# One-hot matrices of token tile 0 moved to ScalarE, and a product and two casts of the routing moved to GpSimd, in an encoder block on one Trainium2 core

## The chip, the core and the metric

The kernel runs on one core of a Trainium2 chip. The metric is the device time of one execution in microseconds (us), the median of the runs shown. The core's engines are TensorE (PE, with its weight loads as PEld), VectorE (DVE), ScalarE (ACT), GpSimd (POOL) and SyncE (SP); each runs its own instructions in the order in which the program lists them and waits for the others by semaphores. A gather of table rows is an indirect DMA that GpSimd issues.

## The reference

One layer: a normalised input goes through two mixers (gated linear attention and differential softmax attention), whose outputs are merged and added. Then comes the part that the change touches, a retrieval layer over 128 x 128 experts, each a row of two tables:

```python
s = einsum('thpc,hpnc->thpn', qb, sub_keys)        # 2 scores per head over 128 keys
sv, si = top_k(s, 16)                              # for each of the two halves
cand = sv[:, :, 0, :, None] + sv[:, :, 1, None, :] # 16 x 16 sums
cidx = si[:, :, 0, :, None] * 128 + si[:, :, 1, None, :]
cv, ci = top_k(cand, 16)
eidx = take_along_axis(cidx, ci)                   # 16 experts of 16384 for a token and head
g = softmax(cv)
a = gelu(einsum('thkd,td->thk', u_tab[eidx], x))   # dot of the token with 16 rows of u
out = einsum('thk,thkd->td', g * a, v_tab[eidx])   # weighted sum of 16 rows of v
```

There are 256 tokens, 8 heads and rows of 2048 numbers, all in 32 bits. Each token so needs 128 rows of each table.

## The kernel before

The 256 tokens are two tiles (`tt` 0 and 1) of 128, one token to a partition. After the mixers come eight `queries(h)`: a projection, scores, and `route(0, h, ...)`, which finds the 16 experts of each token of tile 0 for head h. `route` is a chain of small VectorE instructions: `top16` twice over 128 scores and once over the 256 sums, a cast of the indices (`sif`), shifts and a mask (`hl`), a cast (`hlf`), a comparison that makes one-hot rows (`ohx`, 128x512), a product of these with `sif`, a sum (`ijt`), and the expert's number (`ent`). `route(1, h, ...)` for tile 1 follows in a second loop.

`gather_dots(tt, h, ei)` makes 16 pairs: an indirect DMA on GpSimd that brings one row of the u table to each partition (1 MB), and a VectorE instruction (line 754, "a dot" below) that multiplies it with the tokens and sums. The rows land in buffers of two rings of three, tiles `g` (pool `ring`) and `gr` (tag `raw` of pool `wp`), by turns; a gather waits until the dot that read its buffer last is done. There are 128 gathers and dots for a tile, 256 in all.

`weights_of(tt)` waits for all 128 dots of its tile, applies Gelu on ScalarE, and transposes the expert's numbers and weights to `slotT` (a column for each token). Then 32 calls of `build_w` make W0, a 128x128 matrix for each of the 128 tokens of tile 0, four tokens a call. For a token one engine makes the one-hot row of the first index times the weight (`oi`, VectorE, line 815), another that of the second index (`oj`, GpSimd, line 816), TensorE multiplies the two (line 817), and ScalarE copies four products from PSUM to W0 (line 818). These calls are written after the gathers and dots of tile 1, four calls to a head, and share VectorE's and GpSimd's queues with them. `build_w1` makes W1 for tile 1 later by like means, in part on ScalarE (lines 828 and 829); then W0 and W1 are multiplied with the whole v table (`dense_v`), while 576 of the 2048 columns come by gathers.

The program doesn't set the order of instructions by hand: a scheduler with costs of its own orders each engine's queue when the kernel is built, so that a change of one instruction's engine moves others.

Of the kernel before, what the change touches and what calls it, by code (L numbers as in the profile page):

```python
# [10 lines left out]
F32 = mybir.dt.float32  # L11
# [4 lines left out]
AF = mybir.ActivationFunctionType  # L16
ALU = mybir.AluOpType
# [3 lines left out]
P = 128  # L21
# [19 lines left out]
def block_kernel(ctx: ExitStack, tc: tile.TileContext, A: dict, out: bass.AP):  # L41
    nc = tc.nc

    def pool(name, bufs=1, space=None, side=None, c=ctx):
        kw = {}
        if space is not None:
            kw["space"] = space
        if side is not None:
            kw["side"] = side
        return c.enter_context(tc.tile_pool(name=name, bufs=bufs, **kw))  # L50
# [5 lines left out]
    wp = pool("wp", side="right", c=wpc)  # L56
# [4 lines left out]
    bt = pool("bt")  # L61
# [9 lines left out]
    def pa(shape):  # L71
        return paux.tile(list(shape), F32, tag="pa", name="pa")
# [15 lines left out]
    iota = cc[:, 128:256]  # L88
    onec = cc[:, 256:257]
# [59 lines left out]
    for k in range(KT):  # L149
        ps = pa([P, N])  # L150
# [78 lines left out]
    for kh in range(2):  # L229
        raw = bt.tile([P, 8, 32], F32, tag="ow", name="lraw", bufs=4)  # L230
        nc.sync.dma_start(raw, w_lr[kh])
        hi = wp.tile([P, 8, P], F32R, tag="hi", name="lhi", bufs=3)
# [416 lines left out]
    for j in range(8):  # L649
# [10 lines left out]
        for b in range(2):  # L660
# [3 lines left out]
            for tt in range(2):  # L664
# [4 lines left out]
                                           op1=ALU.subtract)  # L669
# [36 lines left out]
    def top16(vo, io, src, n):  # L706
        tmp = rp.tile([P, n], F32, tag=f"tk{n}", name="tk", bufs=1)
        nc.vector.max(vo[:, 0:8], src)
        nc.vector.max_index(io[:, 0:8], vo[:, 0:8], src)
        nc.vector.match_replace(tmp, vo[:, 0:8], src, NEG)  # L710
        nc.vector.max(vo[:, 8:16], tmp)
        nc.vector.max_index(io[:, 8:16], vo[:, 8:16], tmp)

    def route(tt, h, s_):

        sv = rp.tile([P, 2, 16], F32, tag="sv", name="sv", bufs=2)
        si = rp.tile([P, 2, 16], U32, tag="si", name="si", bufs=2)
        for p in range(2):
            top16(sv[:, p, :], si[:, p, :], s_[:, p, :], P)
        sif = rp.tile([P, 2, 16], F32, tag="sif", name="sif", bufs=2)  # L720
        nc.vector.tensor_copy(sif, si)
        cand = rp.tile([P, 16, 16], F32, tag="cand", name="cand", bufs=1)
        nc.vector.tensor_tensor(cand, sv[:, 0, :].unsqueeze(2).to_broadcast([P, 16, 16]),
                                sv[:, 1:2, :].to_broadcast([P, 16, 16]), op=ALU.add)
        cv = rp.tile([P, 16], F32, tag="cv", name="cv", bufs=2)
        ci = rp.tile([P, 16], U32, tag="ci", name="ci", bufs=2)
        top16(cv, ci, cand.rearrange("p a b -> p (a b)"), 256)
        hl = rp.tile([P, 2, 16], U32, tag="hl", name="hl", bufs=2)
        nc.vector.tensor_scalar(hl[:, 0, :], ci, 4, None, op0=ALU.logical_shift_right)
        nc.vector.tensor_scalar(hl[:, 1, :], ci, 15, None, op0=ALU.bitwise_and)  # L730
        hlf = rp.tile([P, 2, 16], F32, tag="hlf", name="hlf", bufs=2)
        nc.vector.tensor_copy(hlf, hl)
        ohx = rp.tile([P, 2, 16, 16], F32, tag="ohx", name="ohx", bufs=1)
        nc.vector.tensor_tensor(ohx, hlf.unsqueeze(3).to_broadcast([P, 2, 16, 16]),  # L734
                                iota16.unsqueeze(1).unsqueeze(1).to_broadcast([P, 2, 16, 16]), op=ALU.is_equal)
        nc.vector.tensor_tensor(ohx, ohx, sif.unsqueeze(2).to_broadcast([P, 2, 16, 16]), op=ALU.mult)
        nc.vector.tensor_reduce(ij[tt][:, :, h * 16:(h + 1) * 16], ohx, axis=AX.X, op=ALU.add)
        ei = eit[:, tt, h]
        nc.vector.scalar_tensor_tensor(ei, ij[tt][:, 0, h * 16:(h + 1) * 16], 128.0,
                                       ij[tt][:, 1, h * 16:(h + 1) * 16], op0=ALU.mult, op1=ALU.add)  # L740
        nm = rp.tile([P, 1], F32, tag="nm", name="nm", bufs=2)
        nc.vector.tensor_scalar(nm, cv[:, 0:1], -1.0, None, op0=ALU.mult)
        nc.scalar.activation(gw[tt][:, h * 16:(h + 1) * 16], cv, AF.Exp, bias=nm, accum_out=gsum[tt][:, h:h + 1])
        return ei

    def gather_dots(tt, h, ei):
        for k in range(16):
            i = ngather[0]
            ngather[0] += 1
            g = ring.tile([P, D], F32, tag="g", name="g") if i % 2 else wp.tile([P, D], F32, tag="raw", name="gr", bufs=3)  # L750
            nc.gpsimd.indirect_dma_start(out=g, out_offset=None, in_=u_tab,  # L751
                                         in_offset=bass.IndirectOffsetOnAxis(ap=ei[:, k:k + 1], axis=0))
            s = h * 16 + k
            nc.vector.scalar_tensor_tensor(g, g, 1.0, xb[:, tt, :], op0=ALU.mult, op1=ALU.mult,  # L754
                                           accum_out=dots[tt][:, s:s + 1])

    def weights_of(tt):

        rc = rp.tile([P, 8], F32, tag="rcs", name="rcs", bufs=2)
        nc.vector.reciprocal(rc, gsum[tt])  # L760
        g3 = gw[tt].rearrange("p (h k) -> p h k", k=16)
        nc.vector.tensor_mul(g3, g3, rc.unsqueeze(2).to_broadcast([P, 8, 16]))
        nc.scalar.activation(dots[tt], dots[tt], AF.Gelu)
        nc.vector.tensor_mul(gw[tt], gw[tt], dots[tt])  # L764
        ps = pa([P, 3, P])
        nc.tensor.transpose(ps[:, 0, :], ij[tt][:, 0, :], ident)
        nc.tensor.transpose(ps[:, 1, :], ij[tt][:, 1, :], ident)
        nc.tensor.transpose(ps[:, 2, :], gw[tt], ident)  # L768
        r = bt.tile([P, 3, P], F32, tag=f"b{2 + tt}", name=f"slotT{tt}")
        nc.scalar.activation(r, ps, AF.Copy)  # L770
        return r
# [6 lines left out]
    def queries(h):  # L778
        qt = bt.tile([P, 2, T], F32, tag=f"b{2 + h % 2}", name="pqt")

        def ev_pq(b, ps):
            with tc.high_priority():
                nc.scalar.activation(qt[:, b, :], ps, AF.Copy)
        proj(w_q, h * 256, hg, T, ev_pq, lo_eng=nc.vector if h == 0 else nc.gpsimd, ring=wait[h])
        s0 = rp.tile([P, 2, P], F32, tag="sS0", name="sS0", bufs=2)
        with tc.high_priority():
            for tt in range(2):
                ps = pa([P, 2, P])
                for p in range(2):
                    nc.tensor.matmul(ps[:, p, :], lhsT=qt[:, p, tt * P:(tt + 1) * P], rhs=skT[h // 2][:, 2 * (h % 2) + p, :],  # L790
                                     start=True, stop=True)
                nc.scalar.activation(s0 if tt == 0 else sS1[:, h], ps, AF.Copy, scale=rst[tt])
            eis[0, h] = route(0, h, s0)
# [12 lines left out]
    W1E = "pav"  # L806


    def build_w(wt, sT, t4, oj_eng):
        ps = pa([P, 4, P])  # L810
        for q in range(4):
            t = t4 * 4 + q
            oij = bt.tile([P, 2, P], F32, tag="ow", name="oij", bufs=4)
            oi, oj = oij[:, 0, :], oij[:, 1, :]
            nc.vector.tensor_scalar(oi, iota, sT[:, 0, t:t + 1], sT[:, 2, t:t + 1], op0=ALU.is_equal, op1=ALU.mult)
            oj_eng(q).tensor_scalar(oj, iota, sT[:, 1, t:t + 1], None, op0=ALU.is_equal)  # L816
            nc.tensor.matmul(ps[:, q, :], lhsT=oj, rhs=oi, start=True, stop=True)  # L817
        nc.scalar.activation(wt[:, t4 * 4:t4 * 4 + 4, :], ps, AF.Copy)

    def build_w1(vp, wt, sT, nj, t4):  # L820
# [23 lines left out]
    for h in range(8):  # L844
        gather_dots(0, h, eis[0, h])
        eis[1, h] = route(1, h, sS1[:, h])
    w0p = pool("w0p")
    W0 = w0p.tile([P, P, P], F32, name="W0")
    sT0 = weights_of(0)
    for h in range(8):  # L850
        gather_dots(1, h, eis[1, h])
        for t4 in range(4 * h, 4 * h + 4):
            build_w(W0, sT0, t4, lambda q: nc.gpsimd)
    sT1 = weights_of(1)
    ringc.close()
    rgt.close()
# [183 lines left out]
```

## Time and profile before

| | |
|---|---|
| median of 3 runs | 2719.2 us (2715.19 to 2728.39) |
| the profiled execution's own time | 2721.86 us |
| its span in the profile | 2720.1 us |
| busy share of the span | PE 71%, DVE 82%, ACT 37%, POOL 48% |
| mean granted TensorE clock | 0.849 |
| moved by DMA | 659.14 MB, mean 242 GB/s |

Shares are means over the whole span. The routing and the gathers of the u table lie between about 1170 and 2057 us; what an instruction costs there is read from stretches of that time. One dot shows as two instructions in a count, the product (2.29 us) and a short read of the accumulator.

### The profile page before, as it was taken

To read this page: it belongs to the slowest core of one execution; us is meant where nothing else is said; L and a number is where in the kernel's file an instruction comes from. 1 tells how busy PE (TensorE), PEld (TensorE's weight loads), DVE (VectorE), ACT (ScalarE), POOL (GpSimd) and SP (SyncE) were. 2 spreads that over 40 slices of the span, in tenths; PEclk is the share of its full clock that TensorE was granted. 3 is DMA by queue.
4 is the path that set the end of the run, shared out by engine and by line. 5 is a ranking of instruction groups with operands and counts; after the bars stand their busy time and mean duration, and the time that the engine had idled before them with its cause. 6 is when DMAs were issued, how large, how long until landed. Compare 5 with 4: busy or idle time off the path is not lost.

```text
span 2720.1 us, 37043 instructions
## 1 busy us (share of the span) xinstructions
PE 1930.7 (71%) x13809; PEld 1847.4 (68%) x13809; DVE 2236.7 (82%) x3227; ACT 1009.3 (37%) x1790; POOL 1297.3 (48%) x1070
## 2 busy tenths in 40 slices
PE   8999999999999999987000002332006899999997
PEld 7999999999999999977000002221006888888886
DVE  4878887557777765589999997667988999999998
ACT  4555544345555444532000000000006445555444
POOL 1333310001100000076546889999865766667775
PEclk9999999999999999998555555555558899999999
DMA  4444445544444656645999997667993788888886
GB/s 168 142 156 156 167 160 186 186 174 160 163 164 170 218 186 224 225 178 201 344 353 349 363 412 299 212 216 290 421 371 136 256 288 296 298 288 299 289 294 232
DMA packets 111056, 659.14 MB, mean 242 GB/s; under 512 B 14530, under 2 KB 17148, under 8 KB 53260
## 3 DMA queue, kind: packets, MB, share of 16 engines
q0 software_dynamic: 59216, 348.40, 34.7%
q1 hardware_dynamic: 51456, 308.21, 32.6%
q8 instruction: 109, 1.79, 0.3%
q14 instruction: 71, 0.58, 0.1%
q10 hardware_dynamic: 204, 0.17, 0.0%
HBM read 653.53 MB, written 2.10 MB: 241 GB/s over the span
## 4 chain that ended last, share of the span: by engine, by line
DVE 21%; POOL 15%; issue 14%; DMA 3%; PE 3%; ACT 0%; POOLq 0%; DVEq 0%; ACTq 0%
DVE g L754 5%; DVE hs L884 4%; POOL gr L751 3%; POOL oij L816 3%; DVE gr L754 3%; POOL gv L881 3%; POOL g L751 3%; DMA gv<-in_peer_v_dram,ent 2%; POOL vlo L905 2%; PE pa L817 1%; DVE vlo L907 1%; DVE wv L896 1%; DVE oi L839 1%; DVE ohx L734 1%; PE acc L913 1%
## 5 line engine op out<-in xcount | busy, mean ns | idle before, releaser
L186 DVE TENSOR_TENSOR lo<-raw,hi 128x1024 fp32r<-128x1024 f32 x354 | 453.0, 1281 | 243.4 <-ACT hi L185 241.7
L202 PE MATMUL pm<-hT,lo 128*128 128x256 f32 (+1 forms) x2048 | 577.1, 285 | 7.9 <-DVE lo L186 7.9
L200 PE MATMUL pm<-hT,hi 128*128 128x256 f32 (+1 forms) x2048 | 581.2, 285 | 0.0
L201 PE MATMUL pm<-hT,hi 128*128 128x256 f32 (+1 forms) x2048 | 581.0, 284 | 0.0
L185 ACT ACTIVATE hi<-raw 128x1024 fp32r<-128x1024 f32 x374 | 395.6, 1059 | 354.5 <-PE pm L201 285.8
L202 PEld LDWEIGHTS pm<-hT,lo 128*128 128x128 f32 x2048 | 384.2, 189 | 10.7 <-DVE lo L186 9.0
L200 PEld LDWEIGHTS pm<-hT,hi 128*128 128x128 f32 x2048 | 385.4, 188 | 0.3
L201 PEld LDWEIGHTS pm<-hT,hi 128*128 128x128 f32 x2048 | 385.4, 188 | 0.2
L913 PE MATMUL acc<-vlo,wv 128*128 128x368 f32 x1024 | 348.9, 349 | 41.3 <-DVE vlo L905 19.2
L881 POOL DMA_INDIRECT gv<-in_peer_v_dram,ent x256 | 298.1, 1165 | 166.5 <-DVE hs L884 120.1
L768 PE MATMUL pa<-cc,gwt 128*128 128x128 f32 x2 | 1.0, 476 | 466.4 <-DVE gwt L764 466.4
L914 PE MATMUL acc<-vhi,wv 128*128 128x368 f32 x1024 | 331.8, 333 | 0.0
L768 PEld LDWEIGHTS pa<-cc,gwt 128*128 128x128 f32 x2 | 0.4, 183 | 467.1 <-DVE gwt L764 467.1
L754 DVE SCALAR_TENSOR_TENSOR g<-g,xb 128x2048 f32<-128x2048 f32 x128 | 308.0, 2409 | 10.0 <-DMA g<-in_peer_u_dram,ent 9.9
L754 DVE SCALAR_TENSOR_TENSOR gr<-gr,xb 128x2048 f32<-128x2048 f32 x128 | 292.4, 2286 | 21.3 <-DMA gr<-in_peer_u_dram,ent 21.1
L884 DVE SCALAR_TENSOR_TENSOR hs<-gv,gwt,hs 128x576 f32<-128x576 f32 x256 | 289.9, 1133 | 11.7 <-DMA gv<-in_peer_v_dram,ent 11.5
L751 POOL DMA_INDIRECT gr<-in_peer_u_dram,ent x128 | 240.6, 1879 | 97.7 <-DVE gr L754 44.4
L751 POOL DMA_INDIRECT g<-in_peer_u_dram,ent x128 | 236.2, 1845 | 103.3 <-DVE g L754 46.1
L913 PEld LDWEIGHTS acc<-vlo,wv 128*128 128x128 f32 x1024 | 193.3, 190 | 82.9 <-DVE vlo L905 42.4
L895 ACT ACTIVATE wv<-W 128x128 fp32r<-128x128 f32 x256 | 109.7, 430 | 311.6 <-DVE g L754 131.8
L912 PE MATMUL acc<-vhi,wv 128*128 128x368 f32 x1024 | 217.2, 334 | 1.2 <-ACT wv L895 1.1
L914 PEld LDWEIGHTS acc<-vhi,wv 128*128 128x128 f32 x1024 | 193.6, 190 | 0.0
(872 smaller groups left out, 4332.7 us busy)
## 6 DMA issues: line engine op xcount, KB each, us to landing
raw<-in_c_w_in_dram SPq DMA_DIRECT2D x128, 1024.0 KB
raw<-in_c_w_branch_gla_dram SPq DMA_DIRECT2D x16, 1024.0 KB
raw<-in_c_w_branch_diff_dram SPq DMA_DIRECT2D x16, 1024.0 KB
raw<-in_c_w_out_dram SPq DMA_DIRECT2D x16, 1024.0 KB
raw<-in_c_peer_w_q_dram SPq DMA_DIRECT2D x11, 1024.0 KB
gv<-in_peer_v_dram,ent POOLq DMA_INDIRECT x256
raws<-in_c_peer_w_q_dram SPq DMA_DIRECT2D x12, 256.0 KB
xt<-in_x_dram SPq DMA_DIRECT2D x2, 1024.0 KB
```

The lines of the kernel that those rows point to most:

```text
L185: nc.scalar.activation(hi[:, ks], raw, AF.Copy)
L186: (lo_eng or nc.vector).tensor_sub(lo[:, ks], raw, hi[:, ks].bitcast(F32))
L200: nc.tensor.matmul(ps[b], lhsT=wh, rhs=ah, start=(k == 0), stop=False)
L201: nc.tensor.matmul(ps[b], lhsT=wh, rhs=al, start=False, stop=False)
L202: nc.tensor.matmul(ps[b], lhsT=wl, rhs=ah, start=False, stop=(k == KT - 1))
L751: nc.gpsimd.indirect_dma_start(out=g, out_offset=None, in_=u_tab, in_offset=bass.IndirectOffsetOnAxis(ap=ei[:, k:k + 1], axis=0))
L754: nc.vector.scalar_tensor_tensor(g, g, 1.0, xb[:, tt, :], op0=ALU.mult, op1=ALU.mult, accum_out=dots[tt][:, s:s + 1])
L881: nc.gpsimd.indirect_dma_start(out=g, out_offset=None, in_=v_tab, in_offset=bass.IndirectOffsetOnAxis(ap=eis[tt, s // 16][:, s % 16:s % 16 ...
L884: nc.vector.scalar_tensor_tensor(hs[:, tt, DC:], g, gw[tt][:, s:s + 1], hs[:, tt, DC:], op0=ALU.mult, op1=ALU.add)
L912: nc.tensor.matmul(o, lhsT=wh[:, tt, :], rhs=hi[:, ns], start=first(tt), stop=False)
L913: nc.tensor.matmul(o, lhsT=wh[:, tt, :], rhs=lo[:, ns], start=False, stop=False)
L914: nc.tensor.matmul(o, lhsT=wl[:, tt, :], rhs=hi[:, ns], start=False, stop=last(tt))
```

## The change

`build_w`, which was called for tile 0 only, is replaced by `build_w0`. For four tokens ScalarE takes the absolute distance of the index from each column number (8 instructions of 128x128), then one instruction of 128x1024 turns distance 0 into 1 and all else into 0, then four instructions of 128x128 multiply the first one-hot by its weight. The products and the copy to W0 stay. The one-hots of four tokens stand in one tile `oh`, with the tag `hi` of pool `wp` (three buffers). In `route` the two casts and the product of `ohx` with `sif` go from VectorE to GpSimd.

```diff
         sif = rp.tile([P, 2, 16], F32, tag="sif", name="sif", bufs=2)
-        nc.vector.tensor_copy(sif, si)
+        nc.gpsimd.tensor_copy(sif, si)
...
         hlf = rp.tile([P, 2, 16], F32, tag="hlf", name="hlf", bufs=2)
-        nc.vector.tensor_copy(hlf, hl)
+        nc.gpsimd.tensor_copy(hlf, hl)
...
-        nc.vector.tensor_tensor(ohx, ohx, sif.unsqueeze(2).to_broadcast([P, 2, 16, 16]), op=ALU.mult)
+        nc.gpsimd.tensor_tensor(ohx, ohx, sif.unsqueeze(2).to_broadcast([P, 2, 16, 16]), op=ALU.mult)
...
-    def build_w(wt, sT, t4, oj_eng):
+    def build_w0(wt, sT, t4):
         ps = pa([P, 4, P])
+        oh = wp.tile([P, 2, 4, P], F32, tag="hi", name="oh0", bufs=3)
         for q in range(4):
             t = t4 * 4 + q
-            oij = bt.tile([P, 2, P], F32, tag="ow", name="oij", bufs=4)
-            oi, oj = oij[:, 0, :], oij[:, 1, :]
-            nc.vector.tensor_scalar(oi, iota, sT[:, 0, t:t + 1], sT[:, 2, t:t + 1], op0=ALU.is_equal, op1=ALU.mult)
-            oj_eng(q).tensor_scalar(oj, iota, sT[:, 1, t:t + 1], None, op0=ALU.is_equal)
-            nc.tensor.matmul(ps[:, q, :], lhsT=oj, rhs=oi, start=True, stop=True)
+            for a in range(2):
+                nc.scalar.activation(oh[:, a, q], iota, AF.Abs, bias=sT[:, a, t:t + 1], scale=-1.0)
+        nc.scalar.activation(oh, oh, AF.Relu, bias=onec, scale=-1.0)
+        for q in range(4):
+            t = t4 * 4 + q
+            nc.scalar.activation(oh[:, 0, q], oh[:, 0, q], AF.Copy, scale=sT[:, 2, t:t + 1])
+            nc.tensor.matmul(ps[:, q, :], lhsT=oh[:, 1, q], rhs=oh[:, 0, q], start=True, stop=True)
         nc.scalar.activation(wt[:, t4 * 4:t4 * 4 + 4, :], ps, AF.Copy)
```

The scheduler's order moves with it. VectorE's queue behind the weights of tile 0 (line 764; the dots are line 754, the one-hots line 815) was this before:

```order
L764 TENSOR_TENSOR gwt<-gwt 128x128
L754 SCALAR_TENSOR_TENSOR g,gwt<-g,xb 128x2048
L815 TENSOR_SCALAR oij<-cc,slotT_15811 128x128 x4
L754 SCALAR_TENSOR_TENSOR gr,gwt<-gr,xb 128x2048
L815 TENSOR_SCALAR oij<-cc,slotT_15811 128x128 x4
L754 SCALAR_TENSOR_TENSOR g,gwt<-g,xb 128x2048
```

and is this now:

```order
L764 TENSOR_TENSOR gwt<-gwt 128x128
L754 SCALAR_TENSOR_TENSOR g,gwt<-g,xb 128x2048 x2
L754 SCALAR_TENSOR_TENSOR gr,gwt<-gr,xb 128x2048
L754 SCALAR_TENSOR_TENSOR g,gwt<-g,xb 128x2048
L754 SCALAR_TENSOR_TENSOR gr,gwt<-gr,xb 128x2048 x2
L754 SCALAR_TENSOR_TENSOR g,gwt<-g,xb 128x2048 x2
```

The one-hots are gone from between the dots, and in the same way from between the gathers in GpSimd's queue.

ScalarE's queue behind the same place (line 770 writes `slotT`; `oh` are the one-hots of one call each, `W` is W0) now holds the work of three calls side by side, where before it held only the 32 copies to W0:

```order
L770 ACTIVATE slotT_15811<-pa 128x384
L815 ACTIVATE oh_15862<-cc,slotT_15811 128x128 x8
L815 ACTIVATE oh_15882<-cc,slotT_15811 128x128 x8
L815 ACTIVATE oh_15902<-cc,slotT_15811 128x128 x5
L816 ACTIVATE oh_15862<-oh_15862,cc 128x1024
L815 ACTIVATE oh_15902<-cc,slotT_15811 128x128 x3
L816 ACTIVATE oh_15882<-oh_15882,cc 128x1024
L819 ACTIVATE oh_15862<-oh_15862,slotT_15811 128x128 x4
L816 ACTIVATE oh_15902<-oh_15902,cc 128x1024
L819 ACTIVATE oh_15882<-oh_15882,slotT_15811 128x128 x4
L819 ACTIVATE oh_15902<-oh_15902,slotT_15811 128x128 x3
L821 ACTIVATE W_15801<-pa 128x512
```

The copy of the first call (line 821) stands behind the one-hots of the next two, so its products have that time to finish.

In the routing of tile 1 GpSimd's queue, which held nothing but gathers there, now has the casts and the product of a head between them (buffer numbers tell the heads apart):

```order
L732 CAST hlf_15527<-hl_15524 128x32
L721 CAST sif_15599<-si_15586 128x32
L751 DMA gr_15393<-in_peer_u_dram,ent_13686 128x2048
L751 DMA gr_15399<-in_peer_u_dram,ent_13686 128x2048
L736 TENSOR_TENSOR ohx_15529<-ohx_15529,sif_15512 128x512
L751 DMA g_15570<-in_peer_u_dram,ent_13686 128x2048
```

and VectorE's queue, for the same head, has the comparison (line 734) and the sum (line 737) two dots apart, with the product between them now made on the other engine:

```order
L754 SCALAR_TENSOR_TENSOR gr_15381,gwt_13684<-gr_15381,xb_12563 128x2048
L734 TENSOR_TENSOR ohx_15529<-hlf_15527,cc_92 128x512
L711 MAX sv_15672<-tk_15674 128x8
L709 MAX_INDEX ci_15604<-cv_15603,cand_15601 128x8
L710 MATCH_REPLACE tk_15605<-cv_15603,cand_15601 128x256
L742 TENSOR_SCALAR nm_15621<-cv_15603 128x1
L709 MAX_INDEX si_15760<-sv_15759,sS1_13682 128x8 x2
L754 SCALAR_TENSOR_TENSOR g_15552,gwt_13684<-g_15552,xb_12563 128x2048
L712 MAX_INDEX si_15673<-sv_15672,tk_15674 128x8
L754 SCALAR_TENSOR_TENSOR g_15558,gwt_13684<-g_15558,xb_12563 128x2048
L711 MAX cv_15603<-tk_15605 128x8
L737 TENSOR_REDUCE ijt_13683<-ohx_15529 128x2x16
```

The comparison reads the cast that stands two gathers ahead of the product in GpSimd's queue, and the gather just ahead of the product (`gr_15399`) waits for the first dot of these rows (`gr_15381`), three buffers back in its ring.

## Rows read from the trace of the kernel before

**Rows 1.** Windows, all engines: us from:to, length, busy us (instructions), clock, DMA share, GB/s.

```profile
core 0: us, PE busy (x) PEld busy (x) DVE busy (x) ACT busy (x) POOL busy (x), PEclk, DMA share, GB/s
...
1654.30:1876.00 221.70, 85.05 (x259) 64.62 (x259) 149.07 (x223) 20.36 (x35) 212.23 (x174) 0.50 0.63 218
1876.00:1996.00 120.00, 0.00 (x0) 0.00 (x0) 111.02 (x98) 0.00 (x0) 105.37 (x48) 0.50 1.01 417
```

**Rows 2.** Windows, the dots of line 754 alone: length, VectorE's busy us (instructions).

```profile
1654.30:1876.00 221.70, 105.59 (x92) 0.50 0.63 218
1876.00:1996.00 120.00, 111.00 (x97) 0.50 1.01 417
1996.00:2056.70 60.70, 45.09 (x40) 0.50 0.83 314
```

**Rows 3.** Timeline of two dots after W0: start, duration, idle time before.

```profile
1987.76 2.29 DVE L754 SCALAR_TENSOR_TENSOR gr<-gr,xb 128x2048 f32<-128x2048 f32 x1 [0.18 <-DMA gr<-in_peer_u_dram,ent]
1989.98 0.08 DVE L754 DVE_READ_ACCUMULATOR gr<-gr,xb 128x1 f32 x1
1990.23 2.29 DVE L754 SCALAR_TENSOR_TENSOR g<-g,xb 128x2048 f32<-128x2048 f32 x1 [0.16 <-DMA g<-in_peer_u_dram,ent]
```

**Rows 4.** Timeline of one round while W0 is built.

```profile
1662.90 2.29 DVE L754 SCALAR_TENSOR_TENSOR g<-g,xb 128x2048 f32<-128x2048 f32 x1
1662.96 4.45 POOL L816 TENSOR_SCALAR oij<-cc,slotT 128x128 f32<-128x128 f32 x4
...
1667.58 1.01 POOL L751 DMA_INDIRECT gr<-in_peer_u_dram,ent  x1 [0.17 <-DVE oij L815]
...
1668.56 2.29 DVE L754 SCALAR_TENSOR_TENSOR g<-g,xb 128x2048 f32<-128x2048 f32 x1
```

**Rows 5.** Groups of ScalarE instructions, two stretches: busy us, mean ns, idle before.

```profile
L842 ACT ACTIVATE W<-pa 128x512 f32<-128x512 f32 x28 | 16.5, 588 | 3.1 <-PE pa L841 2.0
L828 ACT ACTIVATE oj<-cc,ent 128x128 f32<-128x128 f32 x42 | 14.5, 391 | 2.8 <-PE pa L841 2.5 <-DVE ent L861 0.3
...
L185 ACT ACTIVATE hi<-raw 128x1024 fp32r<-128x1024 f32 x20 | 21.0, 1058 | 16.7 <-PE pm L201 12.8 <-issue 2.6 <-POOL lo L186 1.3
```

**Rows 6.** Groups on VectorE from 1291 to 1563.5 us: what the change moves.

```profile
L736 DVE TENSOR_TENSOR ohx<-ohx,sif 128x512 f32<-128x512 f32 x11 | 7.5, 682 | 0.0
...
L732 DVE CAST hlf<-hl 128x32 f32<-128x32 uint32 x11 | 2.5, 224 | 0.0
...
L721 DVE CAST sif<-si 128x32 f32<-128x32 uint32 x10 | 1.7, 174 | 0.0
```

**Rows 7.** Timeline where VectorE and GpSimd meet, in the projections.

```profile
1229.56 8.12 DVE L734 TENSOR_TENSOR ohx<-hlf,cc 128x512 f32<-128x512 f32 x1
1230.06 7.06 POOL L186 TENSOR_TENSOR lo<-raw,hi 128x1024 fp32r<-128x1024 f32 x3
```

**Rows 8.** Two-input GpSimd instructions of 128x512, by line: least, median, greatest ns.

```profile
L186 POOL TENSOR_TENSOR lo<-raws,hi x12: 1281/1299/3321, 1178.5 to 1227.6; 128x512 fp32r<-128x512 f32 x12
...
L406 POOL TENSOR_TENSOR kif<-kT,e x4: 2271/2283/2290, 78.1 to 314.5; 128x512 f32<-128x512 f32 x4
```

**Rows 9.** Timeline: a gather's issue beside a dot, and small GpSimd copies.

```profile
1402.51 3.02 POOL L751 DMA_INDIRECT g<-in_peer_u_dram,ent  x1 [1.67 <-DVE ent L739]
...
2057.14 0.30 POOL L889 COPY vr__17001<-gwt 128x1 f32<-128x1 f32 x1 [7.29 <-ACT gwt L763]
```

**Rows 10.** Groups on VectorE and GpSimd from 1170 to 1291 us, the projections.

```profile
L754 DVE SCALAR_TENSOR_TENSOR g<-g,xb 128x2048 f32<-128x2048 f32 x14 | 47.7, 3410 | 2.2 <-DMA g<-in_peer_u_dram,ent 2.2
L734 DVE TENSOR_TENSOR ohx<-hlf,cc 128x512 f32<-128x512 f32 x5 | 15.8, 3169 | 0.0
L729 DVE TENSOR_SCALAR hl<-ci 128x16 uint32<-128x16 uint32 x5 | 11.9, 2371 | 0.0
...
L186 POOL TENSOR_TENSOR lo<-raw,hi 128x1024 fp32r<-128x1024 f32 x18 | 42.5, 2383 | 3.2 <-ACT hi L185 3.0
L186 POOL TENSOR_TENSOR lo<-raws,hi 128x512 fp32r<-128x512 f32 x12 | 20.7, 1752 | 3.3 <-ACT hi L185 3.2
```

More of the change, by code (lines that the diff above doesn't have):

```diff
@@ L852, in block_kernel @@
         for t4 in range(4 * h, 4 * h + 4):
-            build_w(W0, sT0, t4, lambda q: nc.gpsimd)
+            build_w0(W0, sT0, t4)
     sT1 = weights_of(1)
```

## The prediction

> **What bounds the kernel now.** I went from the whole to the stretch: first the page's 40 slices, where TensorE is idle and VectorE and the DMA engines are busy from about 1300 to 2050 us; then windows over that time; then the groups and the timeline inside the windows. The stretch that the change rewrites is the building of W0, 1654.3 to 1876 us. There the DMA engines are busy 0.63 of the time, against 1.01 in the stretch behind it, where the same gathers run without one-hots [rows 1]. Counting the dots (two instructions each) gives the pace: 46 dots in 221.7 us, 4.82 us for one, while W0 is built; 48 dots in 120 us behind it, 2.47 us for one; and 20 in the last 60.7 us [rows 2]. In the fast stretch a dot of 2.29 us follows another after 2.47 us, and its short wait is for the gather's data [rows 3]: with the DMA share of 1.01 I read 2.48 us a dot as the floor that the transfers set.
>
> What makes 4.82 us of it is seen in one round [rows 4]. The dot starts at 1662.90; GpSimd's four one-hots start 0.06 us later and take 4.45 us, until 1667.41; only then comes the next gather, at 1667.58, and the next dot at 1668.56. Four such one-hots without a dot beside them would be about 2 us (4.45 less the dot's 2.29), so the first of them stands still until the dot is over. Then VectorE waits for TensorE, which waits for GpSimd. Neither DMA nor VectorE is full; the two engines take turns.
>
> **The W0 half.** It takes 128 one-hots from VectorE, and 128 from GpSimd, out of this chain. What is left there is dots and gathers, which is the stretch behind it. So 46 dots at 2.48 us take 114.1 us instead of 221.7: 107.6 us less. The other 68 dots of this time keep theirs, 180.7 us, the slow end included, where one ring alone is left. The bounds of this term: at the pace of the dots alone without any wait, 2.29 us, it would be 116; if ScalarE's new work slowed the pace to the mean of the last two windows, 180.7/68 = 2.66 us, it would be 99.
>
> This holds if ScalarE hides the building. A call of four tokens has 12 instructions of 128x128, for which the nearest row is the same kind of one-hot in W1, 0.391 us each; one of 128x1024, for which a copy of this size has 1.058 us; and the copy from PSUM, 0.588 us [rows 5]. That is 12 x 0.391 + 1.058 + 0.588 = 6.34 us, and 203 us for 32 calls. ScalarE is otherwise idle there: 20.4 us of 221.7, nearly all of it the copies that stay [rows 1]. The cover is 114.1 + 180.7 = 294.8 us of gathers and dots, so there are 92 us to spare, and up to 9.2 us a call cost nothing. The tags change nothing on the path: `hi` has been free since the projections ended. Behind ScalarE's one-hots in its queue stands only work that needs W0 whole or the last dot.
>
> **The routing half.** It takes from VectorE, for each of 16 heads and tiles, 0.682, 0.224 and 0.174 us [rows 6]. An instruction starts about 0.07 us before the recorded end of the one ahead (1989.98 against 1987.76 + 2.29) [rows 3], so the time given back is 1.08 - 0.21 = 0.87 us, 13.9 us in all. VectorE sets the pace of the routing, so these count.
>
> Against it stands what GpSimd does to VectorE. VectorE's comparison of 128x512 took 8.12 us where GpSimd ran three two-input instructions for 7.06 us beside it [rows 7]: it stood until they were over. In the projections the dots, the comparison and the shift are longer than their normal 2.29, 0.68 and 0.17 us (the first of rows 3, and the same or larger shapes of rows 6) by 15.6 + 12.4 + 11.0 = 39 us, with 63.2 us of such work on GpSimd [rows 10]: 0.62 us lost for each us of it. The trace has no product of this form on GpSimd; two-input instructions of 128x512 take 1.28 us at the least and 2.28 in another place [rows 8]. I take 1.28, the lower, as it is the nearest in time and neighbours. A cast of 128x32 isn't there either; a copy of one column takes 0.30 us [rows 9], and 0.54 us (the 128x128 one-hot, by the remainder above, 2.16/4) bounds it from above; I take 0.3. Together 1.88 us a route, 30 us in all, and at 0.62 that costs 18.6 us. So the half is a loss of 18.6 - 13.9 = 4.7 us. Its bounds: if GpSimd's work always fell beside instructions that don't mind it, a gain of 13.9; if all of it at the upper prices (2.28 + 1.08 = 3.36 us) stopped VectorE, 53.8 - 13.9 = 39.9 us of loss.
>
> The Trainium skill speaks against this half: its page "SBUF — State Buffer", section "SBUF: two separate sides", has VectorE and GpSimd share one pair of ports as an exclusive lock for a whole instruction, and "Perfetto Trace Analysis", section "Optimizing Scalar/DVE Operations", warns that moving work between the two might not help. The 8.12 us comparison agrees with the lock. [...]
>
> New waits: the comparison waits for the cast `hlf`, which stands two gathers and two dots ahead; that is over 4.5 us of dots for a cast, so I cost it at nothing, and without that cover it would be one gather's issue, up to 3.02 us [rows 9]. The sum waits for the product, two dots behind the comparison; the product waits for one gather's issue (3.02 at most), perhaps the rest of a dot, and its own 1.28: 3.02 + 2.29 + 1.28 = 6.6 us against some 6 us of dots and searches. That is nearly covered; I cost it at nothing and keep up to 1 us a route for the range. Behind the sum stand the dots, and behind the product the gathers; these have six buffers, so a gather issued 3 us late is hardly seen.
>
> **The sum.** The profiled execution took 2721.9 us: 2721.9 - 107.6 + 4.7 = 2619.0. That execution lies 2.7 us above the median of the runs shown, which is within their scatter. 0.5% of the time, some 14 us, is about what a measurement of this kernel can tell from no change.
>
> **The rivals.**
> First, the routing loses in earnest: VectorE stopped in full at the upper prices (39.9) and 1 us a route for the late product (16): 2721.9 - 107.6 + 55.9 = 2670. For it: the 2.28 us rows, the head of GpSimd's queue. Against it: the searches and maxima between dots, which take one input and didn't lengthen. Chance 0.20.
>
> Second, ScalarE becomes the bound of W0. If it stood still for TensorE's whole work in each call (85.05 us in 32 calls, 2.66 us each [rows 1]), 6.34 + 2.66 = 9.0 us stays just under 9.2. At 10.5 us a call the building would take 336 us, 41 more than the cover: 2660. For it: the copy to W0 needs the products. Against it: three calls stand side by side in the queue. Chance 0.06.
>
> Third, the routing gains: most of the 13.9 us comes through, and the floor proves nearer the dots' own: 2721.9 - 116 - 10 = 2596. Chance 0.09.
>
> Fourth, slower: in GpSimd's queue the product stands behind gathers that wait for dots, and with VectorE's sum waiting for the product both could stop each other for two gathers and a dot each time: 2 x 3.02 + 2.29 + 2.28 = 10.6 us a route, 170 us in all, and 2721.9 - 107.6 + 170 - 13.9 = 2770. It decides from (107.6 + 13.9)/16 = 7.6 us a route. Against it: the comparison stands behind the dot that frees the gather's buffer. Chance 0.03.
>
> **How the numbers follow.** The forecast has 0.62: 2619 us, from 2602 to 2642 by its own bounds. The range of 8 in 10 reaches to the routing's gain and most of its loss: 2596 to 2664. All cases but the fourth are faster by more than 14 us; between it and them almost nothing lies: faster 0.96, same 0.01, slower 0.03.
>
> **What would show it.** Behind the weights of tile 0, dots every 2.48 us from the first, and no GpSimd instruction but gathers; ScalarE's one-hots at 0.39 us, done some 90 us before the last dot; from there to the last dot 295 us instead of 402. In the routing, the product at 1.3 us on GpSimd, and some dots lengthened by about that. The prediction is wrong if the pace of the dots stays over 2.7 us with ScalarE at work, if W0 is the last to be ready, or if VectorE's sum waits long for the product.

## The result, and the profile after

| | before | after |
|---|---|---|
| median | 2720.36 us (2715.19 to 2728.39, 4 runs) | 2642.18 us (2638.1 to 2647.54, 4 runs) |
| ratio | | 0.9711, 95% interval 0.9681 to 0.9741 |
| the profiled execution, its span | 2721.86, 2720.1 us | 2638.1, 2636.3 us |

The change takes 78 us off the median and 83.8 off the profiled execution, where the prediction had 102.9. The direction and the mechanism are as predicted. The profiled execution lies 19 us above the forecast of 2619, which was reckoned from a profiled execution too, and the median 23 us above it; most of this is found in one place.

The windows of the kernel after, from the weights of tile 0 (1655.7) to the last dot (1974.4), cut where the pace changes (the columns are the window, its length, the busy time of each engine with its instructions, the granted clock, the DMA share and GB/s):

```profile
1655.70:1798.00 142.30, 49.36 (x217) 44.20 (x217) 131.06 (x114) 141.36 (x397) 122.94 (x58) 0.61 1.01 421
1798.00:1822.00 24.00, 9.86 (x42) 9.08 (x42) 1.92 (x5) 21.07 (x55) 1.91 (x2) 0.64 0.41 171
1822.00:1919.00 97.00, 0.00 (x0) 0.00 (x0) 91.61 (x81) 0.00 (x0) 81.31 (x38) 0.50 0.96 394
1919.00:1974.40 55.40, 0.00 (x0) 0.00 (x0) 37.26 (x35) 0.44 (x2) 18.99 (x13) 0.50 0.77 276
```

The first window answers to the first of [rows 1]: the DMA share has gone from 0.63 to 1.01, and ScalarE, nearly idle there before, is busy for 141.36 of 142.3 us. The same windows for line 754 alone give the dots (two instructions each):

```profile
1655.70:1798.00 142.30, 130.87 (x113) 0.61 1.01 421
1798.00:1822.00 24.00, 1.29 (x3) 0.64 0.41 171
1822.00:1919.00 97.00, 91.61 (x81) 0.50 0.96 394
```

113 instructions are 56.5 dots in 142.3 us, 2.52 us each against 4.82 before [rows 2]. So the one-hots did leave the chain. But from 1798 to 1822 VectorE works for 1.92 us, and the DMA share falls to 0.41. The timeline of this stretch says why (start, duration, engine and line, what it does, and in brackets the idle time ahead of it with what ended it):

```profile
1795.86 2.29 DVE L754 SCALAR_TENSOR_TENSOR gr<-gr,xb 128x2048 f32<-128x2048 f32 x1 [0.20 <-DMA gr<-in_peer_u_dram,ent]
1796.37 0.69 ACT L821 ACTIVATE W<-pa 128x512 f32<-128x512 f32 x1
...
1799.27 0.94 POOL L751 DMA_INDIRECT gr<-in_peer_u_dram,ent  x1 [0.30 <-issue]
...
1819.17 0.60 ACT L821 ACTIVATE W<-pa 128x512 f32<-128x512 f32 x1 [1.33 <-PE pa L820]
1819.80 0.76 ACT L898 ACTIVATE wv<-W 128x128 fp32r<-128x128 f32 x2
1820.24 0.71 DVE L899 TENSOR_TENSOR wv<-W,wv 128x128 fp32r<-128x128 f32 x2 [22.08 <-ACT wv L898]
1820.87 2.28 DVE L754 SCALAR_TENSOR_TENSOR g<-g,xb 128x2048 f32<-128x2048 f32 x1
...
1823.43 2.75 POOL L751 DMA_INDIRECT g<-in_peer_u_dram,ent  x1 [23.22 <-DVE g L754]
```

`dense_v` splits a column of W0 into a high part (line 898, ScalarE) and a low part (line 899, VectorE, W0 less the high part). The low parts of the first two columns stand between the dots in VectorE's queue:

```order
L754 SCALAR_TENSOR_TENSOR gr,gwt<-gr,xb 128x2048
L899 TENSOR_TENSOR wv<-W_15801,wv 128x128 x2
L754 SCALAR_TENSOR_TENSOR g,gwt<-g,xb 128x2048
```

They need all of W0, which ScalarE has ready at 1819.8. VectorE comes to them after 1798.1 and stands for 22.08 us; with it stand the dots, which would free the buffers, and so GpSimd's gathers (23.22 us).

ScalarE's groups while it builds W0 (busy time and mean ns of one):

```profile
L815 ACT ACTIVATE oh<-cc,slotT 128x128 f32<-128x128 f32 x256 | 81.2, 443 | 0.1
L819 ACT ACTIVATE oh<-oh,slotT 128x128 f32<-128x128 f32 x128 | 42.2, 448 | 0.0
L816 ACT ACTIVATE oh<-oh,cc 128x1024 f32<-128x1024 f32 x32 | 38.0, 1194 | 0.0
L821 ACT ACTIVATE W<-pa 128x512 f32<-128x512 f32 x32 | 20.3, 633 | 1.4 <-PE pa L820 1.3
```

It waits for 1.4 us in all; the three calls side by side do what they were read to do. W0 is done 164.1 us behind the weights (1655.7 to 1819.8).

In the routing, from the first sum (1180.1) to the weights of tile 0, the groups of GpSimd, and VectorE's sum with the wait ahead of it:

```profile
L736 POOL TENSOR_TENSOR ohx<-ohx,sif 128x512 f32<-128x512 f32 x15 | 27.6, 1843 | 1.5 <-DVE ohx L734 1.3
L732 POOL CAST hlf<-hl 128x32 f32<-128x32 uint32 x15 | 17.1, 1138 | 0.0
L721 POOL CAST sif<-si 128x32 f32<-128x32 uint32 x15 | 13.4, 893 | 0.4 <-DVE si L712 0.4
```
```profile
L737 DVE TENSOR_REDUCE ijt<-ohx 128x32 f32<-128x512 f32 x16 | 10.7, 671 | 2.9 <-POOL ohx L736 2.9
```

The last routing sum starts at 1532.6 where it started at 1563.5 before, but the weights of tile 0 come at 1655.7 against 1654.12: 31 us earlier became 1.6 us later.

### The profile page after: what moved, and what is told of

Its sections match the earlier page's. It is cut to its first block, busy times and chain, and to the rows that moved or that the text cites. A ratio compares the mean times of both kernels' runs of the same rounds, so it can differ in the third digit from the quotient of the medians.

```text
span 2636.3 us, 37183 instructions
## 1 busy us (share of the span) xinstructions
PE 1898.6 (72%) x13809; PEld 1836.1 (70%) x13809; DVE 2180.0 (83%) x3051; ACT 1153.3 (44%) x2206; POOL 1277.3 (48%) x990
## 5 line engine op out<-in xcount | busy, mean ns | idle before, releaser
L884 POOL DMA_INDIRECT gv<-in_peer_v_dram,ent x256 | 320.7, 1253 | 142.7 <-DVE hs L887 95.1
L916 PE MATMUL acc<-vlo,wv 128*128 128x368 f32 x1024 | 341.3, 346 | 44.6 <-DVE vlo L908 29.0
L754 DVE SCALAR_TENSOR_TENSOR g<-g,xb 128x2048 f32<-128x2048 f32 x128 | 326.3, 2553 | 15.4 <-DMA g<-in_peer_u_dram,ent 15.4
L887 DVE SCALAR_TENSOR_TENSOR hs<-gv,gwt,hs 128x576 f32<-128x576 f32 x256 | 303.6, 1186 | 15.3 <-DMA gv<-in_peer_v_dram,ent 14.4
L751 POOL DMA_INDIRECT gr<-in_peer_u_dram,ent x128 | 254.5, 1988 | 81.8 <-DVE gr L754 37.0
L751 POOL DMA_INDIRECT g<-in_peer_u_dram,ent x128 | 250.3, 1956 | 83.1 <-DVE g L754 31.8
```

What stands on the lines that cost most here:

```text
L884: nc.gpsimd.indirect_dma_start(out=g, out_offset=None, in_=v_tab, in_offset=bass.IndirectOffsetOnAxis(ap=eis[tt, s // 16][:, s % 16:s % 16 ...
L887: nc.vector.scalar_tensor_tensor(hs[:, tt, DC:], g, gw[tt][:, s:s + 1], hs[:, tt, DC:], op0=ALU.mult, op1=ALU.add)
L916: nc.tensor.matmul(o, lhsT=wh[:, tt, :], rhs=lo[:, ns], start=False, stop=False)
```

## The experiments

The theory: VectorE's wait for W0 at the early low parts is what the gain lacks, its length being ScalarE's end less the time at which VectorE gets there, and the routing half costs a few us. Its rivals: the routing half hides a large loss or gain; the stall is paid back behind it or in the dense stage; ScalarE's length costs nothing. The times of a set were taken on one chip, beside runs of the kernel before there (2724.91 us in the first set, 2724.02 in the second).

Single executions also differ ahead of the routing. Up to VectorE's first search (line 708) every engine has the same instructions in the same order in all ten profiles, and yet that search starts between 1167.22 and 1174.03 us. So a difference of a few us in such absolute times says nothing about an edit. From the first search to the end of the execution the profiles of one kernel agree far better: 1468.1 and 1468.0 us for the change in its two profiles, against 1551.4 before. This time is given for each experiment below; it rests on one profile of each.

**The W0 half alone.** The three lines of `route` as before:

```diff
-        nc.gpsimd.tensor_copy(sif, si)
+        nc.vector.tensor_copy(sif, si)
-        nc.gpsimd.tensor_copy(hlf, hl)
+        nc.vector.tensor_copy(hlf, hl)
-        nc.gpsimd.tensor_tensor(ohx, ohx, sif.unsqueeze(2).to_broadcast([P, 2, 16, 16]), op=ALU.mult)
+        nc.vector.tensor_tensor(ohx, ohx, sif.unsqueeze(2).to_broadcast([P, 2, 16, 16]), op=ALU.mult)
```

> The W0 half alone: the two casts and the product of the routing are back on VectorE. Theory (the routing half costs about 1.6 us, and the W0 half gives some 80 us, with a stall of about 22 us of VectorE at the early high/low split of W0 inside): ratio to the kernel before 0.970 to 0.971, the weights of token tile 0 ready at about 1654 us, the last dot some 319 us behind them, and the same stall. Rival A, the routing half loses in earnest and hides it before the weights of tile 0: ratio 0.964 or less. Rival B, the routing half gains most of its 13.9 us and the W0 half gives less than it seems: ratio 0.975 or more.

Measured: 2637.16 us, ratio 0.9672 (0.9659 to 0.9684). It lies between the theory and rival A. Its longest wait at the low part is 21.5 us, so the stall belongs to the W0 half and not to the routing. From the first search to the end it took 1465.7 us, 2.4 below the change. The ratios, from different measurements, would make the routing half cost some 10 us, but their intervals overlap; the next runs tell it better.

**The routing half alone**: the same three lines, the other way, in the kernel before.

> The routing half alone, on the kernel before: W0 is built as before on VectorE and GpSimd. Theory: the last routing sum comes some 30 us earlier, the weights of tile 0 within 2 us of 1655.7 us, the W0 stretch keeps its 402 us, ratio 1.000 to 1.002. Rival A, a loss in earnest (GpSimd's products stop VectorE in full): ratio 1.007 or more. Rival B, a gain of the 13.9 us: ratio 0.996 or less.

Measured: 2730.07 us (12 runs), ratio 1.0018 (1.0007 to 1.0029): 4.9 us, with 1.9 to 7.9 by the interval. The theory's 1.000 to 1.002 holds, both rivals fall. The last sum comes at 1535.2, the weights at 1657.04, the last dot 403.9 us behind them; from the first search to the end it took 1554.7 us, 3.2 above the kernel before.

**The early low parts behind the last dot.** One column of the high part is first copied from the dots, so that the split must wait for them:

```diff
         wh, wl = wv[:, 0], wv[:, 1]
+        if i < 3 and tts == (0,):
+            nc.scalar.activation(wh[:, 0, 0:1], dots[1][:, HD:HD + 1], AF.Copy)
```

> The change, with the high parts of the first three splits of W0 made to wait for dot 100 of tile 1 (one column copied from it on ScalarE), so that the low parts stand behind the last dot in VectorE's queue and not among the dots. Theory (the missing 24 us are VectorE's wait for W0 at the early low part): no wait there, 295 to 300 us from the weights of tile 0 to the last dot, ratio 0.962 to 0.964 (about 2619 us). Rival A, the stall was paid back by the six full buffers behind it: 305 us or more, ratio 0.967 or above. Rival B, the dense stage needs the early low parts, and what is saved ahead of it is lost at its start: last dot 22 us earlier, ratio still 0.970 to 0.971.

Measured: 2620.98 us, ratio 0.9619 (0.9605 to 0.9633). The low parts stand behind the last dot (the wait was for all of the dots, not for dot 100 alone). VectorE's longest waits between 1655 and 1960 us are now those for gathers (total, times, longest):

```profile
DVE gr L754 <- DMA gr<-in_peer_u_dram,ent: 19.7, 63, 3.1
DVE g L754 <- DMA g<-in_peer_u_dram,ent: 9.4, 46, 1.1
```

and line 754 in windows from the weights (1655.63) on runs at the pace of the transfers until one ring alone is left:

```profile
1655.60:1715.60 60.00, 55.74 (x49) 0.59 1.01 421
1715.60:1775.60 60.00, 54.61 (x49) 0.61 1.01 421
1775.60:1820.60 45.00, 41.63 (x37) 0.61 1.01 421
1820.60:1855.60 35.00, 32.38 (x29) 0.50 1.01 421
1855.60:1895.60 40.00, 36.16 (x32) 0.50 1.01 422
1895.60:1925.60 30.00, 23.56 (x22) 0.50 0.85 321
```

The last dot ends at 1946.4, 290.8 us behind the weights, where it was 318.7 after the change. From the first search to the end it took 1448.7 us, 19.4 below the change. The theory's total holds, and rivals A and B fall. The last dot is even 4 us ahead of the theory's range, but in this profile 9 of the 28 us are given back behind it (670.9 us to the end, against 662.0).

**One more instruction for ScalarE in each call:**

```diff
         nc.scalar.activation(oh, oh, AF.Relu, bias=onec, scale=-1.0)
+        nc.scalar.activation(oh, oh, AF.Relu)
```

> The change, with one more Relu of 128x1024 in each of the 32 calls on ScalarE (1.19 us each, 38 us in all; it alters no value). The low parts of the early split stand ten dots (25 us) later in VectorE's queue than in the change. Theory (the stall is ScalarE's end of W0 less the time at which VectorE comes to the low part): stall 22 + 38 - 25 = 35 us, the last dot 13 us later, ratio 0.975 to 0.977. Rival A, ScalarE has 92 us to spare and its length costs nothing: ratio 0.970 to 0.972, stall unchanged. Rival B, the pace of the dots itself depends on ScalarE's load: the dots take over 2.6 us in the stretch ahead of the stall.

Measured: 2646.7 us, ratio 0.9713 (0.9699 to 0.9727). The new instruction adds less than its recorded 1.07 us to a call, since neighbours overlap in the records: W0 is ready at 1850.16, 194.2 us behind the weights, 30.1 us later than after the change and not 38. VectorE comes to the low part ten dots later (the split is one line further down in this kernel):

```profile
1821.48 2.29 DVE L754 SCALAR_TENSOR_TENSOR g<-g,xb 128x2048 f32<-128x2048 f32 x1 [0.19 <-DMA g<-in_peer_u_dram,ent]
...
1850.16 0.76 ACT L899 ACTIVATE wv<-W 128x128 fp32r<-128x128 f32 x2
1850.61 0.71 DVE L900 TENSOR_TENSOR wv<-W,wv 128x128 fp32r<-128x128 f32 x2 [26.83 <-ACT wv L899]
```

The ten dots took 25.4 us (the wait begins 167.8 us behind the weights, not 142.5), so the rule gives 22.1 + 30.1 - 25.4 = 26.8 us, and the wait is 26.83. The mechanism holds; my forecast of 35 was off by the 8 us of the overlap, and with it the theory's 13 us for the last dot, which came 2.8 us later, and its ratio. The dots ahead of it kept their pace, 2.5 us (rival B falls). The median can't tell this from rival A, in whose range 0.9713 lies. The wait can, and so can the time from the first search to the end: 1472.9 us, 4.8 above the change, as much as the wait is longer.

**The second set**: the change again, the late low parts again, these with the routing back on VectorE, and the change with a second product on GpSimd, whose diff is

```diff
         nc.gpsimd.tensor_tensor(ohx, ohx, sif.unsqueeze(2).to_broadcast([P, 2, 16, 16]), op=ALU.mult)
+        nc.gpsimd.tensor_tensor(ohx, ohx, onec.unsqueeze(1).unsqueeze(1).to_broadcast([P, 2, 16, 16]), op=ALU.mult)
```

**The change again.**

> The change itself once more, beside the others of this set. Theory: ratio 0.971, as first measured (2642.2 to 2720.4). If the first W0-only run's 0.967 against it is the routing half's price of some 10 us, 0.970 to 0.972 stays; if that difference was scatter between chips, the change comes to 0.968 to 0.969.

Measured: 2641.62 us, ratio 0.9693 (0.9672 to 0.9714), between the two cases; it decides neither.

**The late low parts again.**

> The change with the early low parts of W0 behind the last dot, once more. Theory: 0.962 to its kernel before, some 20 to 24 us below the change of the same set, no long wait of VectorE between the dots. Rival (the dense stage loses again what the dots gain): less than 10 us below the change.

Measured: 2623.3 us, ratio 0.9633 (0.9611 to 0.9654), 18.3 us below the change of the same set: a little under the theory's 20, and nearly twice the rival's bound. From the first search to the end it took 1449.3 us, 18.7 below the change. In this profile the last dot comes 300.1 us behind the weights and the rest takes 662.7 us, so the 9 us that moved behind the last dot in the first profile move between executions of one kernel.

**The late low parts, with the routing back on VectorE.**

> The early low parts behind the last dot, and the routing's casts and product back on VectorE. Theory (the routing half costs 2 to 5 us, the stall is gone): 2 to 5 us below the run with the routing half in, ratio 0.960 to 0.962. Rival A, the routing half costs some 10 us: ratio 0.958 or less. Rival B, without the stall the earlier routing gains: ratio 0.964 or more.

Measured: 2615.89 us, ratio 0.9597 (0.9578 to 0.9617), 7.4 us below the run with the routing half in. The ratio lies between the theory and rival A; rival B falls. This is the fastest version: 4% below the kernel before, and 25.7 us below the change. From the first search to the end it took 1446.1 us, 2.6 and 3.2 below the two profiles with the routing half in.

**The second product.**

> The change, with a second product on GpSimd behind the first in each of the 16 routes (times a column of ones, which alters no value): 16 instructions of 1.3 to 1.8 us, 21 to 29 us of GpSimd more. Theory (VectorE loses 0.62 us for each us of such work): the weights of token tile 0 come 13 to 18 us later, ratio 5 to 7 thousandths above the change. Rival A, GpSimd's work in the routing lies beside dots and searches that don't mind it: 3 us or less. Rival B, VectorE stands still for all of it or waits for the later sum: 21 us or more.

Measured: 2648.17 us, ratio 0.9715 (0.9692 to 0.9737), 6.5 us above the change of the set. The weights come at 1663.29, 7.6 and 9.9 us later than in the two profiles of the change (1655.69 and 1653.43), but this isn't the price of the product: the first search, ahead of any product, is 5.8 and 6.8 us late already. In the two profiles of the change and in this one it starts so:

```profile
1168.22 0.49 DVE L708 MAX8 sv<-sS 128x8 f32<-128x128 f32 x2 [8.49 <-ACT sS L792]
1167.22 0.49 DVE L708 MAX8 sv<-sS 128x8 f32<-128x128 f32 x2 [8.49 <-ACT sS L792]
1174.03 0.49 DVE L708 MAX8 sv<-sS 128x8 f32<-128x128 f32 x2 [11.87 <-ACT sS L793]
```

Also, the scheduler put only 139 dots ahead of the weights, where it puts 142 in the change. From the first search to the end, with all dots inside, it took 1473.3 us, 5.2 above the change. The new product takes longer than I expected, and VectorE's sum now waits for it:

```profile
L737 POOL TENSOR_TENSOR ohx<-ohx,cc 128x512 f32<-128x512 f32 x16 | 35.5, 2221 | 0.9
```
```profile
L738 DVE TENSOR_REDUCE ijt<-ohx 128x32 f32<-128x512 f32 x16 | 10.9, 684 | 15.7 <-POOL ohx L737 15.7
```

So 35.5 us of GpSimd's time cost 5.2 us, 0.15 for one, and less than the 15.7 us that VectorE visibly waits. None of the three forecasts holds: the price is a quarter of the theory's 0.62. Why a wait of VectorE costs less than itself I read in the DMA share between the projections and the last routing sum. The W0-only run, the change and the double product, in this order:

```profile
1300.00:1400.00 100.00, 0.66 (x2) 0.29 (x2) 100.00 (x211) 1.60 (x8) 49.27 (x35) 0.50 0.95 358
1400.00:1500.00 100.00, 0.00 (x0) 0.00 (x0) 100.00 (x197) 1.20 (x6) 56.49 (x33) 0.50 0.94 347
```
```profile
1300.00:1400.00 100.00, 0.66 (x2) 0.29 (x2) 98.14 (x203) 1.20 (x6) 81.28 (x46) 0.50 0.91 342
1400.00:1500.00 100.00, 0.00 (x0) 0.00 (x0) 99.10 (x191) 2.00 (x10) 71.47 (x44) 0.50 0.91 338
```
```profile
1300.00:1400.00 100.00, 0.66 (x2) 0.29 (x2) 95.62 (x194) 1.20 (x6) 87.94 (x51) 0.50 0.89 336
1400.00:1500.00 100.00, 0.00 (x0) 0.00 (x0) 97.10 (x183) 1.60 (x8) 91.84 (x47) 0.50 0.86 326
```

With the routing on VectorE the transfers were at 0.95 already. There is little room for dots to come sooner there, and behind the routing (1.01 from 1566 on in all three) none. A routing that ends earlier leaves more dots behind, at 2.48 us each; what GpSimd's work would cost there is the gathers that it issues late. This reading is argued from the shares; no run has tried it by itself.

## Why the prediction was right and where it was off

**The W0 term** (-107.6 us): right in mechanism, and mis-sized in this kernel. The step that failed is "Behind ScalarE's one-hots in its queue stands only work that needs W0 whole or the last dot". The sentence is true of ScalarE's queue, but the work that needs W0 whole has a partner on VectorE, and that partner stood among the dots. It could have been read from the kernel before, where it stands 46 dots behind the weights with 68 more dots behind it, and waits as W0 becomes ready:

```profile
1875.38 0.71 DVE L896 TENSOR_TENSOR wv<-W,wv 128x128 fp32r<-128x128 f32 x2 [3.01 <-ACT wv L895]
```

There VectorE made the one-hots itself and so came to the low part late. Now it comes 57 dots behind the weights, at the faster pace. So the cover was not the 294.8 us to the last dot: it ended where VectorE reached the low part, some 142 us behind the weights, and with ScalarE at 164 us there were no 92 us to spare but 22 too few. The term measured 402.6 - 318.7 = 83.9 us. With the early low parts moved, the 114.1 + 180.7 = 294.8 us from the weights to the last dot came out as 290.8 and 300.1, and the forecast of 2619 us as 2620.98 and 2623.3: the prediction is the time of the kernel without that wait. Without the routing half as well the time from the first search to the end fell by 105.3 us (1551.4 to 1446.1), close to the 107.6.

**The range**: the measured time lies inside 2596 to 2664, just past the upper edge of the forecast's own 2602 to 2642, but the room there was meant for a loss in the routing, not for a wait at the low part. That the range held is luck. Nor is 2602 to 2642 worked out: the bounds of the two terms together give 2592 to 2663. And the prediction's three signs of being wrong did not catch the miss: the pace was 2.52 us, W0 was ready long before the last dot, and the sum waited little.

**ScalarE's time**: 6.34 us a call was forecast, 5.1 measured (164.1 us less some 1.5 ahead of the first one, in 32 calls), although each instruction of 128x128 is recorded longer than [rows 5] had it, 443 against 391 ns. Forecast "done some 90 us before the last dot"; it was 154.5.

**The routing term** (+4.7 us): right in sign and about right in size. The routing half alone gave 4.9 us, its removal from the faster version 7.4, and the traces from the first search to the end 2.4 to 3.2 us in three comparisons. Its parts were not right. GpSimd's instructions held 58.1 us in 15 routes and not 30 in 16: the product's median of 1.29 us in the profile is the price taken from [rows 8], but its mean is 1.84, and the casts took 0.9 to 1.1 us on average instead of 0.3, since most that start beside a dot stand still until it is over. Here a cast ends 0.06 us behind the dot's own last read:

```profile
1365.36 2.28 DVE L754 SCALAR_TENSOR_TENSOR gr<-gr,xb 128x2048 f32<-128x2048 f32 x1
1365.42 2.29 POOL L721 CAST sif<-si 128x32 f32<-128x32 uint32 x1
1367.57 0.08 DVE L754 DVE_READ_ACCUMULATOR gr<-gr,xb 128x1 f32 x1
```

The 0.54 set as their upper bound was read too low besides: the one-hots that it stands for took 0.59 us at the least and 0.60 as a median (line 816 before). Against this the price per us was a quarter of the 0.62 from [rows 10], as far as the added product can tell. (The 0.62 also leaves out the cast `sif` of that stretch, 7.5 us for six where 0.17 each is normal; with it the price there is 0.72.) At 0.15 the 58.1 us would cost 8.7 us, and only some 6 of the 13.9 us given back would have arrived; both are estimates. Errors cancelled, and that the sum came out near 4.7 is luck. The step behind both is "VectorE sets the pace of the routing": in the projections it may (the DMA share is 0.57 from 1170 to 1300 in the W0-only run), and [rows 10] come from there. After 1300 us, as argued above, the transfers stand so close to their limit that neither VectorE's saved time nor its lost time counts in full.

The Trainium skill's "SBUF — State Buffer", section "SBUF: two separate sides", gives the shared ports for a whole instruction to whichever starts first, a GpSimd instruction that reads SBUF or a VectorE instruction with two inputs in SBUF, and has the other blocked. The lengthened casts agree with that (1.14 us on GpSimd for the cast that VectorE made in 0.25 us in the W0-only run, both on average; a dot has two inputs). What such blocking costs the whole execution is another matter: 0.15 us for each us of the added product here.

**New waits**: costed at nothing; the sum waited 2.9 us and the comparison 1.2 us in all 16 routes. Right.

**Rivals.** A loss of the routing in earnest, a gain of it, and gathers and sums stopping each other did not come. The second, ScalarE as the bound of W0, named the right engine with the wrong end: it was to decide from 9.2 us a call, by the last dot; it decided at 5.1, by an instruction in the middle of another queue.

## What to carry to other kernels

When work moves to another engine, the work that consumes its result can stay about where it was in its own queue (here 57 dots behind the weights, where it was 46). Look for that consumer in the order of the engine that was relieved: the distance from the start of the moved work to that instruction, not to the end of the stage, is the cover that the slower engine has. And before time given back by an engine is counted, look at the DMA share of the same stretch: at 0.95 there was little left to win (argued here, not tried), and a price per us measured in a stretch with a share of 0.6 did not carry over.

## What the runs showed of the hardware

ScalarE's records of neighbouring instructions overlap: after the change eight of 128x128 took 2.55 us from the start of the first to the end of the last, 0.32 us each, with a recorded mean of 443 ns (the timeline at 1806.86, below). A sum of recorded durations was so an upper bound of its time: 7.2 us a call by the means after the change (8 x 0.443 + 4 x 0.448 + 1.194 + 0.633), 5.1 by the clock.

```profile
1806.86 2.55 ACT L815 ACTIVATE oh<-cc,slotT 128x128 f32<-128x128 f32 x8
```

Behind the stall the dots ran for a while at their own pace, with six full buffers, 2.21 us from 1820.87 to 1823.08, so that a stall of 22.1 us was not paid in full: taking it away gave 18.3 us in the medians of the second set, and 18.7 and 19.4 from the first search to the end. What stays open is the routing half's price, 2.4 to 3.2 us in the traces and 4.9 to 7.4 in the medians; the intervals are wide enough for both to be one number. Open is also why the executions reach the first search up to 6.8 us apart.
